# Moving recurrence, layernorm and merge work between engines in a one-core decoder layer

## The chip, the cores and the metric

The kernel runs on one core of one Trainium2 chip. The metric is the device time of one execution in microseconds (us); the profile shows one further execution, taken by the hardware profiler. In profile lines PE is the matmul engine (PEld its weight loads), DVE the vector engine, ACT the activation engine, POOL the GpSimd engine and SP the engine that issues most loads. L158 is line 158 of the kernel before.

## The reference

One layer of a hybrid decoder for 512 prompt tokens and 32 sample tokens (8 sequences of 4), which share all weights. It is computed in float32. The model width is 1024, the hidden width of the MLP 4096.

```python
def _layer(x, states, lp, lb):
    proj = x @ lp["w_in"] + lp["b_in"]          # 15 segments, 51 blocks of 128 columns
    ...
    o, s_gla_new = _gated_linear_scan(q, k, v, g, s_gla)        # 4 heads, dk 48, dv 96
    h_gla = _head_rmsnorm(o, lp["gla_norm_g"]) * jax.nn.silu(gr)
    ...                                                          # mLSTM: 4 heads of 96
    o, s_hg_new = _gated_linear_scan(qh, kh, vh, log_fh, s_hg)  # 4 heads of 64
    h_hg = _head_rmsnorm(o, lp["hg_norm_g"]) * jax.nn.silu(hgt)
    gates = jax.nn.sigmoid(mg)
    merged = (gates[0] * (h_gla @ lp["w_up_gla"]) + gates[1] * (h_ml @ lp["w_up_ml"])
              + gates[2] * (h_hg @ lp["w_up_hg"]))
    x = _layernorm(DN_ALPHA * x + merged @ lp["w_out"], lp["ln1_g"], lp["ln1_b"])
    hid = jnp.square(jax.nn.relu(x @ lp["w_ff_up"]))
    x = _layernorm(DN_ALPHA * x + hid @ lp["w_ff_down"], lp["ln2_g"], lp["ln2_b"])

def _gated_linear_scan(q, k, v, g, s0):          # in chunks, b = cumsum(g)
    rel = exp(where(causal, b[:, :, None] - b[:, None, :], -inf))
    att = sum(q[:, :, None] * k[:, None, :] * rel, axis=-1)
    o = einsum(q * exp(b), s) + einsum(att, v)
    s = exp(b_last) * s + einsum(k * exp(b_last - b), v)
```

## The kernel before, in words

Activations lie with channels on the 128 partitions and the 544 tokens along the free axis, as 8 blocks ("k rows") of 128 channels. Every large product goes through the helper `gemm`. `wload` brings in a weight block of 128 x 1024 as `raw`, ACT copies it to a rounded high part `wh` (L141), and DVE subtracts to get the low part `wl` (L142). For each k row PE then runs three passes (wh with the high activations, wh with the low ones, wl with the high ones), each over two halves of 272 tokens (L158): 48 matmuls for a 1024-deep block. `wh` and `wl` have two buffers each, and so has the PSUM tile `g` of the product. The activations of the layer (`xh`, `xl`), of the MLP's input (`x1h`, `x1l`) and later the last weights (`lh`, `ll`) lie in tiles of `TX` = 546 columns per k row; `x1h` uses the two extra columns for the layernorm's scale and offset.

The program's order is the order of the code, with weight conversion and the emptying of PSUM moved ahead by a priority (`tc.high_priority(OFF)`). It is: the input projections, with the three recurrences run as generators (`together`, `pipe`) whose small matmuls are placed between those of later projections; the three merges, mLSTM first, then GLA, then HGRN2; the output projection with the first layernorm; and twice 16 blocks of the MLP's up product (ff1) followed by its down product (8 output tiles, the last two of which are handled apart at the end, L1066 on).

`gated` is the GLA and HGRN2 recurrence. For each group of tokens, `levels(u)` halves the 128-token chunk again and again: at each level it forms the difference of the cumulative gate `bg` (or `bh`) to the value at the middle of its block, as two subtractions on POOL (L382 for the upper, L384 for the lower half), takes one exponential of the whole tile on ACT (L385), multiplies keys and queries on DVE (L387, L393), lets PE form the scores `lv` (L401) and copies them under a mask into `at` (L405). The diagonal of `at` is written first, from `dps` (PE) over `dsb` (DVE, L364), by one broadcast product on POOL (L367). `sample` brings the states of the eight sample sequences up to date: `spread_v` writes the values eight times under a mask on POOL (L312), POOL scales the state (L503), PE forms `kvs`, DVE adds it (L510).

A `Merge` first runs gate products (`gates`, 48 matmuls each, bias L215, sigmoid in three ACT steps L206 to L208) and then branch products (`products`, 12 matmuls each in the third merge, since HGRN2 has a depth of 256). The product is multiplied by the gate (L868), added to `merged` on POOL (L872), and in the third merge split into `mh` and `ml` for the output projection.

`ln_tile` is called for each of the eight output tiles that a layernorm sums over. It centres on the mean of the first four tiles, before the exact mean and variance are known: tiles 0 to 2 only go into a sum, and at tile 3 PE forms the mean `mu` by a product with `ones5` (1/512), ACT copies it to `cm`, and DVE subtracts it from all four tiles (L972). ACT squares them, POOL adds tile and square to `a1` and `a2` (L978, L979). Later tiles are handled as they come.

Of the kernel before, what the change touches and what calls it, by code (L numbers as in the profile page):

```python
# [42 lines left out]
def build(tc, I, O):  # L43
    nc = tc.nc
    with ExitStack() as ctx:
# [297 lines left out]
        def gated(q, k, b, sc, dv, vtok, sname, nt, gate):  # L343
# [5 lines left out]
            def levels(u):  # L349
# [17 lines left out]
                nc.gpsimd.tensor_tensor(  # L367
                    out=atv, in0=ident[0:R, None, 0:R].to_broadcast([R, 4 * C, R]),
                    in1=dsb[0:R, 0:4 * C, None].to_broadcast([R, 4 * C, R]), op=ALU.mult)

                for li, m in enumerate(LEVELS):
# [10 lines left out]
                    nc.gpsimd.tensor_tensor(out=Ev[:, :, :, m:2 * m], in0=bb[:, :, :, m:2 * m], in1=ref, op=ALU.subtract)  # L382
                    if m > 1:
                        nc.gpsimd.tensor_tensor(out=Ev[:, :, :, 0:m], in0=ref, in1=bb[:, :, :, 0:m], op=ALU.subtract)  # L384
                        nc.scalar.activation(out=E[:, :, 0:L], in_=E[:, :, 0:L], func=AF.Exp, scale=sc)  # L385
                        Kv = K[:, :, 0:L]
                        nc.vector.tensor_tensor(out=blk(Kv)[:, :, :, 0:m], in0=blk(kv)[:, :, :, 0:m], in1=Ev[:, :, :, 0:m], op=ALU.mult)  # L387
                    else:
                        nc.scalar.activation(out=Ev[:, :, :, 1:2], in_=Ev[:, :, :, 1:2], func=AF.Exp, scale=sc)
# [842 lines left out]
```

## Time and profile before

| | us |
|---|---|
| median of 3 runs | 968.91 |
| lowest and highest run | 965.64, 971.26 |
| profiled execution | 968.76 |
| its span (first to last recorded instruction) | 966.9 |
| PE busy | 926.0 (96%) |
| DVE busy | 569.1 (59%) |
| ACT busy | 404.5 (42%) |
| POOL busy | 232.9 (24%) |

The profiled execution's time is the span and 1.9 us around it. The mean granted clock of PE is 0.977 of full speed. PE is busy nearly all the time, so what can be won is the rest: idle stretches of PE, and the time in which its clock is halved behind them. The views used are the page, the groups of instructions by line, the table of stretches (one row per stretch: its start and end, its length, then busy time and count of each engine, the granted clock, the share of the DMA engines and GB/s) and the timeline.

### The profile page before, as it was taken

The page shows a single profiled execution, that of the slowest core. Times are in us where ns is not written, and L with a number is a line of the kernel's source. Part 1 is how long each engine was busy: PE and PEld are TensorE (multiplying, and loading weights), DVE is VectorE, ACT ScalarE, POOL GpSimd, SP SyncE. Part 2 cuts the span into 40 slices and gives each one's busy share as a digit, 9 for nine tenths or more (in the row PEclk, how much of TensorE's full clock was granted, in tenths as well). Part 3 has the DMA queues.
Part 4 walks back from the last instruction along what each step waited for, and adds up shares of the span by engine and source line. Part 5 has one row for each costly group of instructions (what it writes and reads, how often), then busy time and mean ns, then how long its engine had stood idle before and what let it go on. Part 6 is the DMA issues. An engine that isn't in the chain of part 4 may idle for free.

```text
span 966.9 us, 17405 instructions
## 1 busy us (share of the span) xinstructions
PE 926.0 (96%) x7279; PEld 910.7 (94%) x7279; DVE 569.1 (59%) x877; ACT 404.5 (42%) x688; POOL 232.9 (24%) x210
## 2 busy tenths in 40 slices
PE   8999999799999999999989798999999999999795
PEld 7998999799999999999989798999999999999794
DVE  4895467866775676773565855553222455532836
ACT  4386223643555443545523356542111344521414
POOL 0311232643102435120235692000000000001722
PEclk9999999899999999999999899999999999999898
DMA  7321241022132112041144222222222222222202
GB/s 258 118 86 44 84 129 57 16 87 88 60 96 90 49 47 97 25 158 55 33 154 121 79 67 87 88 88 88 87 88 87 88 87 88 88 87 88 85 3 93
DMA packets 37598, 82.73 MB, mean 86 GB/s; under 512 B 12709, under 2 KB 18341, under 8 KB 37521
## 3 DMA queue, kind: packets, MB, share of 16 engines
q1 hardware_dynamic: 25072, 73.28, 23.3%
q10 hardware_dynamic: 12384, 8.33, 3.0%
q8 instruction: 57, 0.93, 0.4%
q14 instruction: 21, 0.16, 0.1%
q0 software_dynamic: 64, 0.02, 0.0%
HBM read 76.51 MB, written 5.09 MB: 84 GB/s over the span
## 4 chain that ended last, share of the span: by engine, by line
PE 86%; DVE 6%; POOL 3%; issue 2%; ACT 1%; DMA 1%; ACTq 0%; DVEq 0%
PE g L158 74%; PE g L83 3%; PE lv L401 2%; POOL merged L1050 2%; POOL merged L1049 1%; DVE wl L142 1%; DVE qe L393 1%; DVE merged L972 1%; PE o L458 1%; DVE x1l L1013 1%; PE oTm L760 1%; PE qkp L673 0%; PE oT L282 0%; DVE ml L180 0%; DMA fw<-in_wfirst 0%
## 5 line engine op out<-in xcount | busy, mean ns | idle before, releaser
L142 DVE TENSOR_TENSOR wl<-raw,wh 128x1024 fp32r<-128x1024 f32 (+2 forms) x139 | 168.4, 1212 | 152.4 <-ACT wh L141 149.6
L141 ACT ACTIVATE wh<-raw 128x1024 fp32r<-128x1024 f32 (+2 forms) x139 | 133.3, 959 | 277.0 <-PE g L158 258.8
L158 PE MATMUL g<-xh,wh 128*128 128x272 f32 x752 | 162.1, 295 | 0.0
L158 PE MATMUL g<-xh,wl 128*128 128x272 f32 x752 | 161.2, 293 | 0.0
L158 PE MATMUL g<-xl,wh 128*128 128x272 f32 x752 | 161.1, 294 | 0.0
L158 PEld LDWEIGHTS g<-xl,wh 128*128 128x128 f32 x752 | 120.8, 191 | 0.9 <-issue 0.5
L158 PEld LDWEIGHTS g<-xh,wh 128*128 128x128 f32 x752 | 121.0, 192 | 0.7 <-issue 0.2
L158 PEld LDWEIGHTS g<-xh,wl 128*128 128x128 f32 x752 | 121.1, 192 | 0.3
L158 PE MATMUL g<-x1h,wh 128*128 128x272 f32 (+1 forms) x512 | 107.1, 290 | 2.9 <-DVE relu L1036 2.9
L158 PE MATMUL g<-x1l,wh 128*128 128x272 f32 (+1 forms) x512 | 106.9, 290 | 0.0
L158 PE MATMUL g<-x1h,wl 128*128 128x272 f32 (+1 forms) x512 | 106.9, 290 | 0.0
L158 PEld LDWEIGHTS g<-x1h,wh 128*128 128x128 f32 x512 | 81.2, 189 | 3.3 <-DVE relu L1036 3.3
L158 PEld LDWEIGHTS g<-x1l,wh 128*128 128x128 f32 x512 | 81.5, 190 | 0.1
L158 PEld LDWEIGHTS g<-x1h,wl 128*128 128x128 f32 x512 | 80.8, 188 | 0.0
L961 POOL TENSOR_TENSOR a<-merged 128x544 f32<-128x544 f32 x2 | 4.8, 2421 | 295.6 <-ACT wh L141 284.3
L158 PE MATMUL g<-hidl,wh 128*128 128x272 f32 x280 | 58.1, 289 | 0.0
L158 PE MATMUL g<-hidh,wh 128*128 128x272 f32 x280 | 57.9, 288 | 0.0
L158 PE MATMUL g<-hidh,wl 128*128 128x272 f32 x280 | 57.8, 288 | 0.0
L1038 ACT ACTIVATE relu<-relu,gw 128x544 f32<-128x544 f32 x32 | 24.0, 750 | 77.2 <-DVE relu L1037 77.2
L872 POOL TENSOR_TENSOR merged<-merged,gb 128x544 f32<-128x544 f32 x16 | 26.8, 1678 | 86.8 <-ACT gb L207 47.8
L215 DVE TENSOR_SCALAR gb<-g,vec 128x544 f32<-128x544 f32 x24 | 18.8, 782 | 45.2 <-PE g L158 45.1
L158 PEld LDWEIGHTS g<-hidl,wh 128*128 128x128 f32 x280 | 44.0, 188 | 0.0
(405 smaller groups left out, 1863.3 us busy)
## 6 DMA issues: line engine op xcount, KB each, us to landing
raw<-in_wff SPq DMA_DIRECT2D x64, 512.0 KB, 3.6
raw<-in_win SPq DMA_DIRECT2D x47, 512.0 KB, 3.2
xr<-in_xT SPq DMA_DIRECT2D x16, 272.0 KB, 3.2
raw<-in_wout SPq DMA_DIRECT2D x8, 512.0 KB, 4.0
out_yT<-merged SPq DMA_DIRECT2D x8, 272.0 KB, 2.4
fw<-in_wfirst ACTq DMA_DIRECT2D x8, 256.0 KB, 5.4
raw<-in_wup_ml SPq DMA_DIRECT2D x8, 192.0 KB, 2.3
raw<-in_wup_gla SPq DMA_DIRECT2D x8, 192.0 KB, 2.4
```

The source lines that it names most:

```text
L83: nc.tensor.matmul(first_ps[i][hf], w[:, i * 128:(i + 1) * 128], a[:, k, hf * HT:(hf + 1) * HT], start=(k == 0 and n == 0), stop=(k == KD ...
L141: nc.scalar.activation(out=h[:, 0:n], in_=raw[:, 0:n], func=AF.Copy)
L142: nc.vector.tensor_tensor(out=l[:, 0:n], in0=raw[:, 0:n], in1=h[:, 0:n].bitcast(F32), op=ALU.subtract)
L158: nc.tensor.matmul(ps[:, hf, 0:w_], w, a(k)[:, hf * HT:hf * HT + w_], start=(k == 0 and s == 0), stop=(k == nk - 1 and s == 2))
L215: nc.vector.tensor_scalar(out, ps, vcol(col), XMIN, ALU.add, ALU.max)
L393: nc.vector.tensor_tensor(out=Q[s, :, p, 0:L // 2].rearrange("p a (n m) -> p a n m", m=m), in0=blk(qv)[s, :, :, m:2 * m], in1=Ev[s, :, :, ...
L401: nc.tensor.matmul(lv[0:R, o:o + 2 * H].rearrange("p (a b) -> p a b", a=2), Kv[:, p, c * R:(c + 1) * R], Q[:, p, :, c * H:(c + 1) * H], st ...
L458: nc.tensor.matmul(o[:, h * dv:(h + 1) * dv], at[:, c * 4 + h, :], vtok[:, cc, h * dv:(h + 1) * dv], start=(h == 0), stop=(cc == 0 and h = ...
L760: nc.tensor.matmul(oT[0:97, h * 32 + 4 * n:h * 32 + 4 * n + 4], Cs[:, n, :], qF[h][:, 4 * n:4 * n + 4], start=False, stop=(h == 3 and n == 7))
L872: eng.tensor_tensor(out=merged[:, m, :], in0=merged[:, m, :], in1=g, op=ALU.add)
L1038: nc.scalar.activation(out=r_, in_=r_, func=AF.Relu, bias=gw[:, 1:2])
L1050: nc.gpsimd.tensor_tensor(out=y, in0=y, in1=rstd, op=ALU.mult)
```

## The change: what it does

1. **Recurrences.** In `levels`, one DVE subtraction over the whole tile takes the place of POOL's two, and the two halves go through two exponentials on ACT, of opposite scale. The diagonal of `at` is written by eight ACT copies (four for the sample tokens), each a 128 x 128 identity scaled by a column of `dsb`. In `sample`, `spread_v` is done by eight ACT copies, and the state is scaled and added to in one DVE instruction per sequence in place of POOL's product and DVE's sum. mLSTM's own calls of `spread_v` stay on POOL.
2. **Layernorms.** They centre on the mean of the first tile alone (`ones7`, 1/128). From tile 0 on every tile is centred when it comes, and the sums `a1`, `a2` are formed on DVE.
3. **Tail.** `ADDP`, `MULP`, `AFFD` are empty: the last additions and products are all on DVE, the last scale and offset all on ACT.
4. **Rows.** `TX` goes from 546 to 548 columns: a k row is 2192 in place of 2184 bytes long.
5. **Third merge.** Gate and branch products alternate, one of each, with one gate ahead, in place of eight gates followed by eight products.

```diff
-TX = T + 2
+TX = T + 4
...
-ADDP, MULP, AFFD = (5, 6, 7), (7,), (2, 5)
+ADDP, MULP, AFFD = (), (), ()
...
-        def spread_v(v, n):
+        def spread_v(v, n, act=False):
             vx = t1.tile([96, 8 * 97], F32R, tag="vx", name="vx", bufs=VXB)
+            if act:
+                for j in range(8):
+                    nc.scalar.activation(out=vx[:, j * n:(j + 1) * n], in_=v.bitcast(F32), func=AF.Copy, scale=bm[0:96, j:j + 1])
+                return vx
...
-                nc.gpsimd.tensor_tensor(
-                    out=atv, in0=ident[0:R, None, 0:R].to_broadcast([R, 4 * C, R]),
-                    in1=dsb[0:R, 0:4 * C, None].to_broadcast([R, 4 * C, R]), op=ALU.mult)
+                for j in range(4 * C):
+                    nc.scalar.activation(out=at[0:R, j, 0:R], in_=ident[0:R, 0:R], func=AF.Copy, scale=dsb[0:R, j:j + 1])
...
-                    nc.gpsimd.tensor_tensor(out=Ev[:, :, :, m:2 * m], in0=bb[:, :, :, m:2 * m], in1=ref, op=ALU.subtract)
                     if m > 1:
-                        nc.gpsimd.tensor_tensor(out=Ev[:, :, :, 0:m], in0=ref, in1=bb[:, :, :, 0:m], op=ALU.subtract)
-                        nc.scalar.activation(out=E[:, :, 0:L], in_=E[:, :, 0:L], func=AF.Exp, scale=sc)
+                        ref2 = bb[:, :, :, m - 1:m].to_broadcast([128, 2, n, 2 * m])
+                        nc.vector.tensor_tensor(out=Ev, in0=bb, in1=ref2, op=ALU.subtract)
+                        nc.scalar.activation(out=Ev[:, :, :, 0:m], in_=Ev[:, :, :, 0:m], func=AF.Exp, scale=-sc)
+                        nc.scalar.activation(out=Ev[:, :, :, m:2 * m], in_=Ev[:, :, :, m:2 * m], func=AF.Exp, scale=sc)
...
+                        nc.vector.tensor_tensor(out=Ev[:, :, :, 1:2], in0=bb[:, :, :, 1:2], in1=ref, op=ALU.subtract)
...
-                    nc.gpsimd.tensor_tensor(
-                        out=Ss[:, :, 0:dv], in0=Ss[:, :, 0:dv],
-                        in1=P[:, p, 0:32].rearrange("p (n m) -> p n m", m=4)[:, :, 3:4].to_broadcast([128, 8, dv]), op=ALU.mult)
...
-                        nc.vector.tensor_tensor(
-                            out=Ss[:, n0:n0 + nb, 0:dv], in0=Ss[:, n0:n0 + nb, 0:dv],
-                            in1=kvs[:, 0:nb * dv].rearrange("p (a b) -> p a b", a=nb), op=ALU.add)
+                        for n in range(n0, n0 + nb):
+                            nc.vector.scalar_tensor_tensor(
+                                Ss[:, n, 0:dv], Ss[:, n, 0:dv], P[:, p, 4 * n + 3:4 * n + 4],
+                                kvs[:, (n - n0) * dv:(n - n0 + 1) * dv], ALU.mult, ALU.add)
...
-        mr_.gates(0, gbp)
-        mr_.gates(4, gb2p)
+        mr_.gates(0, gbp, 1)
         mr_.split()
-        mr_.products(0)
-        mr_.products(4)
-        gb2s.close()
+        for m in range(KD):
+            if m + 1 < KD:
+                mr_.gates(m + 1, gbp, 1)
+            mr_.products(m, 1)
...
-        def ln_tile(x, m, sl, last, after):
+        def ln_tile(x, m, sl, after):
             if m == 0:
-                return
...
+                xr_ = ftile("a1r").bitcast(F32R)
+                nc.scalar.activation(out=xr_[:, sl], in_=x[:, 0, sl], func=AF.Copy)
                 for hf in range(2):
...
+                    nc.tensor.matmul(ps[:, 0:HT], ones7, xr_[:, s], start=True, stop=True)
                     nc.scalar.activation(out=cm[:, s], in_=ps[:, 0:HT], func=AF.Copy)
...
+            nc.vector.tensor_tensor(out=x[:, m, sl], in0=x[:, m, sl], in1=cm[:, sl], op=ALU.subtract)
+            sq = ftile("sq") if m else a2
+            nc.scalar.activation(out=sq[:, sl], in_=x[:, m, sl], func=AF.Square)
+            if after:
+                after(m, sl)
+            if m:
+                nc.vector.tensor_tensor(out=a1[:, sl], in0=x[:, 0, sl] if m == 1 else a1[:, sl], in1=x[:, m, sl], op=ALU.add)
+                nc.vector.tensor_tensor(out=a2[:, sl], in0=a2[:, sl], in1=sq[:, sl], op=ALU.add)
```

The next lists show the order of instructions on one engine, with each row's line, operation, output and inputs, shape and, where it repeats, a count. Rows of the changed kernel carry its own line numbers.

PE before, where GLA's levels for the first 256 tokens begin: `lv` are scores of a level, `oTs` belongs to the sample states, `g` is a projection.

```order
L158 MATMUL g<-xl,wh 128x272 x2
L158 MATMUL g<-xh,wl 128x272
L401 MATMUL lv<-qe_2105,ke_2103 128x128 x4
L489 MATMUL oTs<-at,gvt 96x32 x4
L401 MATMUL lv<-qe_2106,ke_2104 128x128 x4
L498 MATMUL oTs<-qx,Ss 96x2x4 x16
L401 MATMUL lv<-qe_2105,ke_2103 128x128 x4
L158 MATMUL g<-xh,wl 128x272
```

The same place of PE in the changed kernel:

```order
L158 MATMUL g<-xh,wh 128x272
L406 MATMUL lv<-qe_2105,ke_2103 128x128 x4
L158 MATMUL g<-xh,wh 128x272
L158 MATMUL g<-xl,wh 128x272 x2
L158 MATMUL g<-xh,wl 128x272 x2
L158 MATMUL g<-xh,wh 128x272 x2
L158 MATMUL g<-xl,wh 128x272
L494 MATMUL oTs<-at,gvt 96x32 x4
L406 MATMUL lv<-qe_2106,ke_2104 128x128 x4
L503 MATMUL oTs<-qx,Ss 96x2x4 x16
L158 MATMUL g<-xl,wh 128x272
L158 MATMUL g<-xh,wl 128x272 x2
```

Three levels' scores stood behind one another with no projection between them; now projection matmuls stand between them.

DVE before, at tile 3 of the second layernorm: `merged` is the layer's output under way, `a1r` the sum of four tiles that `mu` is formed from, `ll` the last weights.

```order
L1060 TENSOR_TENSOR merged<-merged,g 128x544
L961 TENSOR_TENSOR a1r<-a_5672,merged 128x544
L142 TENSOR_TENSOR wl<-raw,wh 128x1024
L972 TENSOR_TENSOR merged<-merged,cm 128x544 x4
L1075 TENSOR_TENSOR merged<-merged,cm 128x544 x2
L180 TENSOR_TENSOR ll<-raw,lh 128x1024
L142 TENSOR_TENSOR wl<-raw,wh 128x1024
```

DVE in the changed kernel from tile 0 of the second layernorm on:

```order
L1053 TENSOR_TENSOR merged<-merged,g 128x544
L142 TENSOR_TENSOR wl<-raw,wh 128x1024
L965 TENSOR_TENSOR merged<-merged,cm 128x544
L1068 TENSOR_TENSOR merged<-merged,cm 128x544 x2
L142 TENSOR_TENSOR wl<-raw,wh 128x1024
L1053 TENSOR_TENSOR merged<-merged,g 128x544
L965 TENSOR_TENSOR merged<-merged,cm 128x544
L142 TENSOR_TENSOR wl<-raw,wh 128x1024
L971 TENSOR_TENSOR a_5780<-merged 128x544
L972 TENSOR_TENSOR a_5781<-a_5781,sq 128x544
L142 TENSOR_TENSOR wl<-raw,wh 128x1024
```

The block of seven instructions between two weight conversions is gone; at most three now stand there.

DVE in the changed kernel, third merge (before, all L215 with their 1024-wide L142 came first, and then rows such as the last three):

```order
L215 TENSOR_SCALAR gb<-g,vec 128x544
L142 TENSOR_TENSOR wl<-raw,wh 128x1024
L871 TENSOR_TENSOR gb<-g,gb 128x544
L142 TENSOR_TENSOR wl<-raw,wh 128x256
L180 TENSOR_TENSOR ml<-merged,mh 128x544
```

The weight conversion for a gate now falls into the time of a 12-matmul product.

More of the change, by code (lines that the diff above doesn't have):

```diff
@@ L123, in build @@
         nc.gpsimd.memset(epsl, LN_EPS)
-        ones5 = const.tile([128, 128], F32R, name="ones5")
-        nc.gpsimd.memset(ones5.bitcast(F32), 1.0 / 512.0)
+        ones7 = const.tile([128, 128], F32R, name="ones7")
+        nc.gpsimd.memset(ones7.bitcast(F32), 1.0 / 128.0)
         onesn = const.tile([128, 128], F32, name="onesn")
@@ L501, in sample @@
                     yield
-                    vxs = [spread_v(v3[:, (2 * p + e) * dv:(2 * p + e + 1) * dv], dv) for e in range(2)]
-                    nc.gpsimd.tensor_tensor(
-                        out=Ss[:, :, 0:dv], in0=Ss[:, :, 0:dv],
-                        in1=P[:, p, 0:32].rearrange("p (n m) -> p n m", m=4)[:, :, 3:4].to_broadcast([128, 8, dv]), op=ALU.mult)
+                    vxs = [spread_v(v3[:, (2 * p + e) * dv:(2 * p + e + 1) * dv], dv, True) for e in range(2)]
                     for n0 in range(0, 8, nb):
@@ L845, in __init__, with gates @@
                 self.ready = []
-            def gates(self, m0, pl):
-                for m in range(m0, m0 + 4):
+            def gates(self, m0, pl, n=4):
+                for m in range(m0, m0 + n):
                     c = M_G + self.br * KD + m
@@ L861, in split, with products @@
                         split(self.hh[:, k, :], self.hl[:, k, :], self.h[:, k, :])
-            def products(self, m0):
-                for m in range(m0, m0 + 4):
+            def products(self, m0, n=4):
+                for m in range(m0, m0 + n):
                     ps = gemm([(I[self.wup][m], self.nk)], lambda k: self.hh[:, k, :], lambda k: self.hl[:, k, :])
@@ L966, in ln_tile @@
                     s = slice(hf * HT, (hf + 1) * HT)
-                    nc.tensor.matmul(ps[:, 0:HT], ones5, to[:, s], start=True, stop=True)
+                    nc.tensor.matmul(ps[:, 0:HT], ones7, xr_[:, s], start=True, stop=True)
                     nc.scalar.activation(out=cm[:, s], in_=ps[:, 0:HT], func=AF.Copy)
-                nc.gpsimd.memset(a1, 0.0)
-                nc.gpsimd.memset(a2, 0.0)
-            for i in range(0 if m == 3 else m, m + 1):
-                nc.vector.tensor_tensor(out=x[:, i, sl], in0=x[:, i, sl], in1=cm[:, sl], op=ALU.subtract)
-                sq = ftile("sq")
-                nc.scalar.activation(out=sq[:, sl], in_=x[:, i, sl], func=AF.Square)
-                if after:
-                    after(i, sl)
-                eng = nc.vector if last else nc.gpsimd
-                eng.tensor_tensor(out=a1[:, sl], in0=a1[:, sl], in1=x[:, i, sl], op=ALU.add)
-                eng.tensor_tensor(out=a2[:, sl], in0=a2[:, sl], in1=sq[:, sl], op=ALU.add)
+            nc.vector.tensor_tensor(out=x[:, m, sl], in0=x[:, m, sl], in1=cm[:, sl], op=ALU.subtract)
[6 more added lines that the diff above has]
+                nc.vector.tensor_tensor(out=a2[:, sl], in0=a2[:, sl], in1=sq[:, sl], op=ALU.add)
         def ln_sums(hf, stop=True):
@@ L1019, in build @@
             nc.vector.scalar_tensor_tensor(halves(x1[:, m, :]), halves(xr), ALPHA, ps, ALU.mult, ALU.add)
-            ln_tile(x1, m, slice(0, T), m == KD - 1, put_x1)
+            ln_tile(x1, m, slice(0, T), put_x1)
         for hf in range(2):
@@ L1060, in build @@
                     nc.vector.tensor_tensor(out=xm, in0=xm, in1=ps, op=ALU.add)
[L1061 removed]
+                    ln_tile(x1, m, slice(0, T), None)
         lh = bigp.tile([128, KD, TX], F32R, tag="big", name="lh").rearrange("p a b -> p (a b)")
```

8 lines of the change are left out of this document (removed).

## The prediction

> **What bounds the kernel now.** I read the page's totals first, then the table of stretches where PE's busy share drops, then the timeline around each drop.
>
> ```profile
> span 966.9 us, 17405 instructions
> PE 926.0 (96%) x7279; PEld 910.7 (94%) x7279; DVE 569.1 (59%) x877; ACT 404.5 (42%) x688; POOL 232.9 (24%) x210
> PE 86%; DVE 6%; POOL 3%; issue 2%; ACT 1%; DMA 1%; ACTq 0%; DVEq 0%
> ```
>
> PE is the bound. Of the chain that ended last only 14% lies on others, so what any engine can save is PE's idle time and what its clock loses behind that. Stretches (start and end, length, then busy time and count per engine, granted clock):
>
> ```profile
> 170.00:195.00 25.00, 19.66 (x160) 19.02 (x160) 21.94 (x32) 13.83 (x30) 14.65 (x14) 0.80 0.03 9
> 325.00:345.00 20.00, 18.72 (x148) 17.84 (x148) 17.07 (x28) 7.94 (x15) 12.21 (x13) 0.83 0.04 11
> 470.00:500.00 30.00, 24.84 (x177) 23.81 (x177) 22.35 (x29) 12.12 (x23) 12.95 (x9) 0.94 0.33 105
> 530.00:550.00 20.00, 14.72 (x95) 14.31 (x94) 18.08 (x15) 6.48 (x9) 16.06 (x11) 0.83 0.30 93
> 575.00:595.00 20.00, 17.14 (x133) 16.69 (x132) 11.38 (x11) 14.69 (x23) 12.19 (x8) 1.00 0.23 77
> 895.00:920.00 25.00, 19.48 (x134) 19.26 (x133) 22.44 (x16) 9.67 (x14) 18.97 (x11) 0.86 0.27 85
> 430.00:470.00 40.00, 40.00 (x318) 40.00 (x317) 13.11 (x14) 20.51 (x28) 0.00 (x0) 1.00 0.16 54
> 600.00:645.00 45.00, 45.00 (x356) 45.00 (x355) 24.48 (x32) 22.25 (x37) 0.00 (x0) 1.00 0.30 94
> 700.00:745.00 45.00, 45.00 (x361) 45.00 (x360) 12.68 (x12) 8.49 (x8) 0.00 (x0) 1.00 0.27 83
> ```
>
> The last three are undisturbed: 40/318 = 0.126 us per matmul. A stretch of product matmuls alone loses its length less 0.126 x count: the third merge (470 to 500) 7.7 us, the first layernorm (530 to 550) 8.0, the start of ff1 (575 to 595) 3.2, the second layernorm (895 to 920) 8.1. What PE waited for there, in brackets:
>
> ```profile
> 190.52 2.05 PE L401 MATMUL lv<-qe,ke 128*128 128x128 f32 x8 [5.34 <-DVE at L405]
> 336.61 2.07 PE L401 MATMUL lv<-qe,ke 128*128 128x128 f32 x8 [1.28 <-DVE qe L393]
> 491.37 0.52 PE L158 MATMUL g<-mh,wl 128*128 128x272 f32 x2 [2.08 <-DVE wl L142]
> 538.94 0.49 PE L158 MATMUL g<-mh,wh 128*128 128x272 f32 x2 [3.83 <-DVE merged L1019]
> 541.13 0.82 PE L158 MATMUL g<-mh,wl 128*128 128x272 f32 x2 [1.45 <-DVE wl L142]
> 912.99 0.82 PE L158 MATMUL g<-hdh,wl 128*128 128x272 f32 x2 [5.52 <-DVE wl L142]
> ```
>
> The two recurrence stretches mix shapes, so I take gap plus clock. A granted 0.80 over 25 us is 10.0 us at half rate. PE stood for 5.34 of them; the other 4.7 cost half, 2.3; sum 7.7. At 325 to 345 it is 6.8 us at half, 1.28 idle, 2.7 for the rest; sum 4.0. The stretches the change touches hold 7.7 + 4.0 + 7.7 + 8.0 + 8.1 = 35.5 us.
>
> All these waits end on DVE, and in both layernorms DVE was slow while POOL added up tiles (its share of these stretches is in the table above):
>
> ```profile
> 899.82 4.97 DVE L972 TENSOR_TENSOR merged<-merged,cm 128x544 f32<-128x544 f32 x4 [2.42 <-ACT cm L968]
> 904.72 3.68 DVE L1075 TENSOR_TENSOR merged<-merged,cm 128x544 f32<-128x544 f32 x2
> 908.32 2.35 DVE L180 TENSOR_TENSOR ll<-raw,lh 128x1024 fp32r<-128x1024 f32 x1
> 910.59 2.35 DVE L142 TENSOR_TENSOR wl<-raw,wh 128x1024 fp32r<-128x1024 f32 x1
> 914.66 1.21 DVE L142 TENSOR_TENSOR wl<-raw,wh 128x1024 fp32r<-128x1024 f32 x1
> 541.00 0.71 DVE L972 TENSOR_TENSOR merged<-merged,cm 128x544 f32<-128x544 f32 x1
> ```
>
> The same L142 takes 2.35 and 1.21 us, L1075 1.84 each against 0.71 for a like L972. So two things make the layernorm's stall: a block of seven instructions ahead of one `wl`, and POOL's additions beside it.
>
> **Second layernorm (gain 7.6 of 8.1, range 5 to 8.1).** Tile 0's centring no longer waits for tile 3, and no block forms. Each tile of two 1024-deep units is 96 matmuls, 12.1 us, and asks DVE for two `wl` (2.4), the emptying L1060 (0.7 by the like L972) and three subtractions or sums (3 x 0.71): 5.3 us. At tile 0 L1075 comes on top (1.4, without POOL). The new thing at tile 0, the product for `mu`, stands behind the evacuation and an ACT copy; PE has 35 product matmuls (4.4 us) ahead of it, against 0.7 + 0.65 for the two. Lower end 5: another short gap with 3 us of half clock.
>
> **First layernorm (gain 7.5 of 8.0, range 4 to 8).** Tiles are 48 matmuls, 6.03 us. DVE per tile: `wl` 1.21, and L1019, the centring, L1013 and two sums at 0.71 each, by the like shape: 4.8 us, 80% busy, so it keeps up without POOL. The `mu` product has 18 matmuls (2.3 us) of cover.
>
> **Third merge (gain 3 of 7.7, range 0 to 7.7).** Before, eight 12-matmul products of 1.5 us followed one another, each with an L868, a split and a `wl` on DVE; that is gone, since 60 matmuls (7.5 us) now stand for each pair. But a gate's 1024-wide weights can only be converted into the buffer that the gate before it has released, and PE then has just 12 matmuls:
>
> ```profile
> L141 ACT ACTIVATE wh<-raw 128x1024 fp32r<-128x1024 f32 x115 | 121.7, 1058 | 245.4 <-PE g L158 227.3 <-issue 6.4 <-POOL cvo L584 6.3
> L974 ACT ACTIVATE sq<-merged 128x544 f32<-128x544 f32 x14 | 8.9, 649 | 20.0 <-DVE merged L972 18.6 <-POOL a L979 1.3
> ```
>
> [...] PE needs `wl` after 12 + 4 matmuls at 2.1. A stall of 0.55 for each of 6 gates and a like one ahead of the first output block, with 0.4 of aftermath, are 4.3 us, and 7.7 - 4.3 leaves about 3.
>
> **Recurrences (gain 6 of 7.7 and 2 of 4.0; range 0 to 7.7 and -2 to 4).** What POOL did and what takes its place:
>
> ```profile
> L382 POOL TENSOR_TENSOR E<-bg 128x256 f32<-128x256 f32 x14 | 11.1, 798 | 21.9 <-PE oT L282 11.7 <-DVE kw L797 3.4 <-PE dps L361 2.9
> L384 POOL TENSOR_TENSOR E<-bg 128x256 f32<-128x256 f32 x12 | 8.5, 723 | 0.4
> L367 POOL TENSOR_TENSOR at<-ident,dsb 128x1024 f32<-128x1024 f32 x4 | 7.9, 1974 | 9.5 <-DVE dsb L364 9.5
> L416 DVE TENSOR_TENSOR W<-bg 128x512 f32<-128x512 f32 x2 | 1.4, 684 | 0.0
> L389 ACT ACTIVATE E<-E 128x256 f32<-128x256 f32 x4 | 1.7, 428 | 0.0
> L385 ACT ACTIVATE E<-E 128x512 f32<-128x512 f32 x24 | 14.6, 622 | 4.2 <-POOL E L384 4.1
> L699 ACT ACTIVATE D<-dp,cols 128x128 f32<-128x128 f32 x16 | 4.7, 368 | 16.1 <-PE g L158 12.3 <-PE dp L696 3.8
> L474 DVE SCALAR_TENSOR_TENSOR S<-S,P,kvp 64x96 f32<-64x96 f32 x12 | 3.8, 314 | 3.5 <-PE kvp L466 3.2
> ```
>
> Per level 798 + 723 = 1.52 us on POOL and 0.62 on ACT become 0.68 on DVE and 0.86 on ACT: 0.6 us shorter. The diagonal's copies take 8 x 0.294 (16 of L699 in 4.7 us) = 2.35 against 1.97 before. DVE gains 24 x 0.68 + 4 x 0.4 = 18 us of E and, for 32 state updates at about 0.3 against six sums, 6 us; ACT gains 24 x 0.23 + 40 copies for `at` and 64 for `vx` at 0.27 = 34 us. Averaged over the recurrences both have room, and DVE gets back what POOL took from it, as L142 did above. Around 185 us the order now puts 36 projection matmuls instead of 21 between `dps` and the first `lv`, and 8 or 9 behind it, so the chain is covered by 4.5 us and the spacing of levels by 1.1 us. Hence most of the 7.7 goes; at HGRN2, whose gap is small, I take half. Behind it I charge 2 us (0 to 8) for new short waits, where DVE runs up to four E in a row (2.7 us) ahead of a `wl`.
>
> [...]
>
> **Aligned rows (gain 2.5, range 0 to 4.4).** The three undisturbed stretches have 125.8 ns per matmul on `xh` (430 to 470), 126.4 on `x1h` (600 to 645, of which 0.5 are the extra columns) and 124.7 on `hidh` (700 to 745), whose own rows were 2176 bytes, a multiple of 16.
>
> ```profile
> L158 PE MATMUL g<-xh,wh 128*128 128x272 f32 x752 | 162.1, 295 | 0.0
> L158 PE MATMUL g<-x1h,wh 128*128 128x272 f32 (+1 forms) x512 | 107.1, 290 | 2.9 <-DVE relu L1036 2.9
> ```
>
> Excess 1.1 ns on 3 x 752 and 1.2 on 3 x 512 matmuls: 4.4 us if rows of 2184 bytes are the whole cause. Only every second row starts off a multiple of 16, so I take about half. [...]
>
> **ff1 start and tail (0; tail 1 either way).** ff1's stall hangs on POOL's L1049 and L1050, which stay. In the tail
>
> ```profile
> 955.59 4.02 DVE L1099 TENSOR_TENSOR merged<-merged,ne 128x272 f32<-128x272 f32 x5
> 959.53 2.54 DVE L1103 TENSOR_TENSOR merged<-merged,rstd 128x272 f32<-128x272 f32 x7
> 960.00 3.14 ACT L1107 ACTIVATE merged<-merged,vec 128x272 f32<-128x272 f32 x6 [3.31 <-DVE merged L1103]
> ```
>
> five additions beside POOL took 4.02; eight at L1103's 0.36 take 2.9, eight products follow, and eight ACT steps at 0.52 trail them by 4.2 from about 958.9: they end near 963.1, as before.
>
> **Sum.** 7.6 + 7.5 + 3 + 6 + 2 + 2.5 - 2 = 26.6. The profiled execution is 968.76, within 0.2 of the median 968.91, so 968.76 - 26.6 = 942.2, and I say 942.
>
> **Rivals.**
> - *The recurrences keep their stalls.* `at`'s copies queue on ACT behind sigmoids and `wh`, and two more exponentials per level lengthen the chain. For it: the 2.35 against 1.97. Against it: the shorter E and the added cover. Without the 8: 950. Chance 0.2.
> - *The third merge gives everything back.* If each transition stalls 1 us, eight cost 8: gain 0, so 945. Chance 0.1.
> - *All goes.* All 35.5, the rows at their most: 968.8 - 35.5 - 2.5 to 4.4 = about 930. Chance 0.12.
> - *Slower.* DVE becomes the limit of the recurrences: four E and one half E (3.1 us) ahead of an evacuation and `wl`, where only one 18-matmul product (2.3 us) covers them. One such stall costs 1.9 us and up to 2.7 of half clock, 4.6. The other parts bring 20.6, so from the fifth on the kernel loses and from the sixth it ends above 973.6. DVE's 21.94 of 25 us busy in the stretch from 170 speaks for it; that POOL's share leaves that number speaks against. At seven: 980. Chance 0.03.
> - *No effect.* POOL is not what slows DVE, and what moves to DVE takes what the order wins: 966 to 969. The two durations of L142 speak against it. Chance 0.03.
>
> The rest, 0.52, is the forecast. Its own range is 936 to 948; the range that should hold the time goes from all gone with the rows at their most (929) to the first rival with the new waits at their full 8 us (956). A measurement of this kernel tells about 0.5%, 4.8 us, from no change: faster (under 964) 0.94, same 0.03, slower 0.03.
>
> **What would show it.** Right: no gap above 1 us in the two layernorms, granted clock near 1.00 there, L142 and the centring at 1.21 and 0.71 throughout; six short gaps <-DVE wl of about 0.5 us in the third merge; at GLA's start a gap under 1 us; pitch on `xh` near 125. Wrong: gaps released by E subtractions or `at`'s copies in the recurrences, or a granted clock still at 0.8 there, would put the time at 950 or over; a stall of 1 us or more per gate in the merge adds 4; L142 still above 2 us with POOL idle would undo the layernorm steps.

## The result, and the profile after

The changed kernel takes 938.39 us, the median of 4 runs (938.21 to 940.08), against 967.27 for the kernel before in the same series: a ratio of 0.970, 95% interval 0.9664 to 0.9737. It is 28.9 us faster; 942 had been forecast, 26.6 us. A second series gave 936.67, ratio 0.9682 (0.9658 to 0.9707), and is the one that the experiments below stand beside. The profiled execution took 940.08, the highest of the four. In the later series two single executions were far slower (2279.04 us of the kernel before, 1485.51 of the last kernel, at a granted clock of 0.554), and the ratios below leave them out.

The page of the changed kernel (totals, then shares of the chain that ended last):

```profile
span 938.2 us, 17454 instructions
PE 916.5 (98%) x7279; PEld 900.4 (96%) x7279; DVE 556.8 (59%) x959; ACT 437.4 (47%) x824; POOL 101.1 (11%) x92
PE 86%; DVE 5%; POOL 3%; ACT 3%; DMA 1%; issue 1%; POOLq 0%; ACTq 0%; DVEq 0%
```

POOL's work fell by 132 us and ACT's rose by 33. DVE took over whole groups of work, and its busy time still fell by 12: what it no longer loses beside POOL pays for what it took. Its `wl` of 1024 columns went from 1310 to 1270 ns in the mean, the layernorms' centring from 1232 to 723.

The table of stretches of the changed kernel (start and end, length, busy time and count per engine, granted clock): GLA's start, HGRN2's start, a place near 370 that was undisturbed before, the third merge up to the first output block, the first layernorm, the start of ff1, the second layernorm.

```profile
170.00:195.00 25.00, 25.00 (x196) 24.41 (x195) 19.62 (x40) 23.23 (x61) 0.20 (x1) 0.86 0.08 25
325.00:345.00 20.00, 20.00 (x176) 19.21 (x176) 16.77 (x38) 14.30 (x41) 0.00 (x0) 1.00 0.12 32
365.00:375.00 10.00, 8.26 (x71) 7.78 (x70) 7.37 (x14) 5.23 (x13) 4.02 (x3) 1.00 0.29 100
428.00:484.00 56.00, 53.60 (x414) 52.06 (x413) 27.45 (x37) 28.45 (x46) 9.66 (x7) 1.00 0.25 82
485.00:535.00 50.00, 50.00 (x400) 50.00 (x400) 35.62 (x47) 20.63 (x28) 1.71 (x1) 1.00 0.40 125
555.00:575.00 20.00, 16.83 (x132) 16.40 (x131) 12.36 (x12) 12.88 (x21) 14.16 (x8) 1.00 0.25 77
840.00:915.00 75.00, 75.00 (x596) 74.84 (x595) 32.93 (x41) 18.73 (x24) 0.00 (x0) 1.00 0.23 71
```

Both layernorms are now seamless at full clock: 400 matmuls in 50 us and 596 in 75. GLA's start has no idle time left, yet its clock is still 0.86 over 25 us. The start of ff1 is as it was. The gaps that remain in these stretches:

```profile
372.74 0.52 PE L158 MATMUL g<-xh,wl 128*128 128x272 f32 x2 [1.74 <-DVE wl L142]
432.64 0.52 PE L158 MATMUL g<-xh,wl 128*128 128x272 f32 x2 [0.16 <-DVE wl L142]
483.19 0.52 PE L158 MATMUL g<-mh,wl 128*128 128x272 f32 x2 [1.44 <-DVE wl L142]
565.08 0.52 PE L158 MATMUL g<-x1h,wh 128*128 128x272 f32 x2 [1.57 <-DVE relu L1029]
572.99 0.52 PE L158 MATMUL g<-x1h,wh 128*128 128x272 f32 x2 [1.60 <-DVE relu L1029]
```

The first is new. The second is one of six in the third merge, 0.16 each. The third is the step to the first output block, and there a `wl` again stands beside a POOL addition (the timelines of DVE and POOL near it):

```profile
479.80 0.72 DVE L871 TENSOR_TENSOR gb<-g,gb 128x544 f32<-128x544 f32 x1 [0.21 <-PE g L158]
480.69 1.37 POOL L875 TENSOR_TENSOR merged<-merged,gb 128x544 f32<-128x544 f32 x1 [6.11 <-DVE gb L871]
480.76 3.52 DVE L142 TENSOR_TENSOR wl<-raw,wh 128x1024 fp32r<-128x1024 f32 x2 [0.24 <-ACT wh L141]
```

Of the two `wl` in 3.52 us, the first took 2.38, with POOL's addition beside it from 480.69 to 482.06; the second, behind it, took 1.21.

### The profile page after: what moved, and what is told of

It is laid out like the page before. It is cut to its first block, busy times and chain, and to the rows that moved or that the text cites. A ratio compares the mean times of both kernels' runs of the same rounds, so it can differ in the third digit from the quotient of the medians.

```text
span 938.2 us, 17454 instructions
## 1 busy us (share of the span) xinstructions
PE 916.5 (98%) x7279; PEld 900.4 (96%) x7279; DVE 556.8 (59%) x959; ACT 437.4 (47%) x824; POOL 101.1 (11%) x92
## 4 chain that ended last, share of the span: by engine, by line
PE 86%; DVE 5%; POOL 3%; ACT 3%; DMA 1%; issue 1%; POOLq 0%; ACTq 0%; DVEq 0%
PE g L158 73%; PE lv L406 3%; PE g L83 2%; DVE wl L142 2%; POOL merged L1043 1%; ACT wh L141 1%; POOL merged L1042 1%; DMA Cs<-in_mC 1%; PE o L463 1%; POOL cvo L586 1%; PE oTs L503 1%; PE oTm L763 1%; PE qkp L676 0%; DMA fw<-in_wfirst 0%; PE oT L282 0%
## 5 line engine op out<-in xcount | busy, mean ns | idle before, releaser
L142 DVE TENSOR_TENSOR wl<-raw,wh 128x1024 fp32r<-128x1024 f32 (+2 forms) x139 | 158.1, 1138 | 144.0 <-ACT wh L141 142.2
L158 PE MATMUL g<-xh,wh 128*128 128x272 f32 x752 | 159.8, 292 | 0.0
L158 PEld LDWEIGHTS g<-hidh,wl 128*128 128x128 f32 x280 | 43.9, 188 | 0.0
L158 PEld LDWEIGHTS g<-hidh,wh 128*128 128x128 f32 x280 | 43.8, 188 | 0.0
L410 DVE COPY_PREDICATED at<-lmask,lv 128x512 f32<-128x512 int32 (+1 forms) x32 | 26.2, 819 | 22.2 <-PE lv L406 18.2
```

What stands on the lines that cost most here:

```text
L142: nc.vector.tensor_tensor(out=l[:, 0:n], in0=raw[:, 0:n], in1=h[:, 0:n].bitcast(F32), op=ALU.subtract)
L158: nc.tensor.matmul(ps[:, hf, 0:w_], w, a(k)[:, hf * HT:hf * HT + w_], start=(k == 0 and s == 0), stop=(k == nk - 1 and s == 2))
L410: nc.vector.copy_predicated(atv.rearrange("p h (n m) -> p h n m", m=2 * m)[:, :, :, m:2 * m], lmask[0:R, li, 0:H].rearrange("p (n m) -> p ...
```

## The experiments

Differences are to the changed kernel's 936.67 (ratio 0.9682). The runs come from four series, in which the kernel before took 969.10, 967.44, 967.74 and 968.33 us, so a difference of 1 or 2 us can come from the series alone. Two kernels whose intervals overlap are not told apart by their times alone; the traces then say which stretch moved.

| kernel | median us | ratio to before (95%) | difference |
|---|---|---|---|
| changed kernel again | 936.67 | 0.9682 (0.9658 to 0.9707) | 0 |
| rows of 546 columns | 941.04 | 0.9718 (0.9695 to 0.9741) | +4.4 |
| third merge in its old order | 940.66 | 0.9721 (0.9695 to 0.9746) | +4.0 |
| recurrences on POOL | 943.13 | 0.9743 (0.9719 to 0.9768) | +6.5 |
| layernorms as before | 953.39 | 0.9860 (0.9836 to 0.9883) | +16.7 |
| first-tile mean, sums on POOL | 939.95 | 0.9717 (0.9689 to 0.9745) | +3.3 |
| four-tile mean, sums on DVE | 942.38 | 0.9747 (0.9724 to 0.9771) | +5.7 |
| small matmuls spread | 962.71 | 0.9952 (0.9934 to 0.9970) | +26.0 |
| only the subtractions on POOL | 934.62 | 0.9661 (0.9636 to 0.9685) | -2.1 |
| small matmuls in two groups | 936.40 | 0.9678 (0.9651 to 0.9705) | -0.3 |
| own weight tiles, POOL affine | 933.91 | 0.9648 (0.9624 to 0.9673) | -2.8 |
| the two that helped, together | 932.55 | 0.9637 (0.9610 to 0.9665) | -4.1 |

### The changed kernel again

> The changed kernel once more, as the reference for the runs beside it. Expected at its earlier median, 938.4 us, within 1 us; the profiled execution earlier was 940.1.

It came out 1.7 us lower than in the first series; single runs lay between 935.0 and 940.6. The section on the hardware comes back to this spread.

### One part undone at a time

```diff
-TX = T + 4
+TX = T + 2
```

> The changed kernel with rows of 546 columns (2184 bytes) again, all else kept. My theory, from the traces: a matmul on the x tiles whose row starts off a multiple of 16 bytes is slower. The changed kernel's trace has 753 to 755 ns per six matmuls on every row of xh, the one before 765 on every second; over 188 such rows of xh and 128 of x1h that is 11 ns x 316 = 3.5 us, and 0.5 for the rest: slower by about 4 us, 942. The prediction's term was 2.5. Rival: the pitch follows something else (what POOL or the loads do beside it), and the rows are worth nothing: 938 to 939, with all rows alike in the trace.

Measured +4.4, and the rival falls. The same two stretches of both kernels, the changed one first, have 323 against 320 and 320 against 317 matmuls in 40 us:

```profile
25.00:65.00 40.00, 40.00 (x323) 39.96 (x322) 34.60 (x67) 23.27 (x48) 8.66 (x6) 1.00 0.34 110
590.00:630.00 40.00, 40.00 (x320) 40.00 (x319) 22.32 (x28) 19.53 (x34) 0.00 (x0) 1.00 0.29 89
```
```profile
25.00:65.00 40.00, 40.00 (x320) 39.96 (x320) 34.42 (x68) 23.09 (x48) 8.42 (x6) 1.00 0.34 111
590.00:630.00 40.00, 40.00 (x317) 40.00 (x316) 20.55 (x26) 20.92 (x35) 0.00 (x0) 1.00 0.26 82
```

That is 125.0 against 126.2 ns in the second; 1.2 ns over 3792 matmuls are 4.5 us.

```diff
-        mr_.gates(0, gbp, 1)
+        mr_.gates(0, gbp)
+        mr_.gates(4, gb2p)
         mr_.split()
-        for m in range(KD):
-            ...
+        mr_.products(0)
+        mr_.products(4)
```

> The changed kernel with the third merge in its old order (eight gates, then eight products), all else kept. My theory: the old order loses what it lost before, 7.7 us between the last gate and the first output block, against 2.2 in the new order, so slower by 5.5 us: 944. The prediction's term was 3. Rival: part of the old loss came from POOL work and ran into DVE, which is relieved elsewhere, and the short products keep PE fed now: slower by 0 to 2 us.

Measured +4.0, between the two; the spans of the profiled executions differ by 2.5 us only (938.6 against 936.1), so the size is uncertain. The old gaps are back, 0.96, 0.98, 1.03 and 2.09 us, released by `wl` and by L871 as they were before. The stall comes with the order.

```diff
-                        nc.vector.tensor_tensor(out=Ev, in0=bb, in1=ref2, op=ALU.subtract)
-                        ... (two exponentials, eight copies for the diagonal, spread on ACT, eight state updates)
+                    nc.gpsimd.tensor_tensor(out=Ev[:, :, :, m:2 * m], in0=bb[:, :, :, m:2 * m], in1=ref, op=ALU.subtract)
+                        ... (all as in the kernel before)
```

> The changed kernel with the recurrences' work back on POOL (both subtractions, the diagonal, the spread and the state's scaling), all else kept. My theory: both recurrence starts stall again, 14 us lost there before against 5.4 now, but the 1.7 us stall that the changed kernel has near 371 goes: slower by 6 to 8 us, 945. The prediction's terms were 6 + 2 - 2. Rival: the first gap depends on how the order of the projections falls and not on POOL, and the two traces differ by that: slower by less than 3 us or by more than 10.

Measured +6.5. GLA's gap is back to within 0.02 us, as the timeline of PE in this kernel shows, and the gap near 370 is gone:

```profile
191.14 2.04 PE L405 MATMUL lv<-qe,ke 128*128 128x128 f32 x8 [5.36 <-DVE at L409]
```

### Which half of the layernorm's change mattered

> The changed kernel with both layernorms as before (mean of four tiles, catch-up at tile 3, sums on POOL), all else kept. My theory: the two stalls that the trace of before showed come back in full, 8.0 and 8.1 us, so slower than the changed kernel's 936.7 by 15 to 16: 952. Rival: a part of the two stalls was owed to rows or to the state that the recurrences leave, and less than 12 comes back.

Both layernorms as before: +16.7. The gaps of the kernel before stand again, 3.85 and 0.95 in the first, 5.54 in the second. Then each half alone, first the sums on POOL, with the new centring:

```diff
-                nc.vector.tensor_tensor(out=a1[:, sl], ...
-                nc.vector.tensor_tensor(out=a2[:, sl], ...
+                nc.gpsimd.tensor_tensor(out=a1[:, sl], ...
+                nc.gpsimd.tensor_tensor(out=a2[:, sl], ...
```

> The changed kernel, centred on the first tile, but with the sums of both layernorms on POOL again. It parts the two causes that the prediction named, the block at tile 3 and POOL beside DVE. If the block made the stalls: no gap comes back, DVE operations beside POOL take up to twice as long (1.21 to 2.35 for a weight conversion) but DVE has 6.03 us per tile for 3.4 us of work, so at most 1 us slower: 937 to 938. If POOL's company made them: gaps before products in both layernorms, slower by 5 us or more.

No gap came back. Stretches of this kernel, for the first and second layernorm:

```profile
485.00:535.00 50.00, 50.00 (x401) 50.00 (x399) 32.70 (x33) 20.44 (x28) 26.31 (x14) 1.00 0.43 124
840.00:915.00 75.00, 75.00 (x593) 74.68 (x592) 26.43 (x29) 18.49 (x24) 17.78 (x10) 1.00 0.22 71
```

POOL works for 26 of 50 us and PE does not stand. The median is 3.3 us higher, with overlapping intervals, while the profiled span is only 0.8 longer (936.9 against 936.1); whether the sums on POOL cost anything is left open. At the start of ff1 this trace has one gap of 2.15 us in place of two gaps, and the mean granted clock of the execution is 0.989 against 0.991. Then the old centring with the sums on DVE (shown against the layernorms of the kernel before):

```diff
-                eng = nc.vector if m == 3 else nc.gpsimd
+                eng = nc.vector
...
-                eng = nc.vector if last else nc.gpsimd
+                eng = nc.vector
```

> The changed kernel with the four-tile mean and the catch-up at tile 3, but all sums on DVE, none on POOL. If the block makes the stalls: at tile 3 of the first layernorm four tiles of centring, low parts and sums (4 x 2.8 us) stand in DVE's queue, more than a tile's 6.03 us, and at the second 4 x 2.1 us ahead of a weight conversion, so gaps of 2 us and more come back with half clock behind them: slower by 8 to 16, 945 to 953. If POOL's company made them: slower by less than 4.

My expectation for the block fell. At +5.7 the kernel is slower, but not at tile 3: PE has no gap there. DVE's timeline at the second layernorm's tile 3 is the same block as before, with one of the sums in it, at about half the time:

```profile
882.46 2.63 DVE L974 TENSOR_TENSOR merged<-merged,cm 128x544 f32<-128x544 f32 x4 [2.50 <-ACT cm L970]
885.01 1.36 DVE L1077 TENSOR_TENSOR merged<-merged,cm 128x544 f32<-128x544 f32 x2
886.28 0.72 DVE L980 TENSOR_TENSOR a<-a,merged 128x544 f32<-128x544 f32 x1
886.91 1.22 DVE L180 TENSOR_TENSOR ll<-raw,lh 128x1024 fp32r<-128x1024 f32 x1
888.05 1.22 DVE L142 TENSOR_TENSOR wl<-raw,wh 128x1024 fp32r<-128x1024 f32 x1
```

From `cm` to the end of the `wl` it takes 6.8 us (882.46 to 889.27); in the kernel before it took 13.1 (899.82 to 912.94). PE had been fed for 7.7 us behind the arrival of `cm` (899.82 to 907.48). So 6.8 fits and 13.1 does not: the stall needed the block and POOL's company, and either half of the change alone takes it away. What this kernel loses instead is a gap of 2.92 us at the start of ff1, with 3.4 us at half clock behind it (pairs of matmuls start 0.45 us apart from 548.1 to 550.9, where 0.25 is usual); that the late sums of the first layernorm hold up `ne` there is the likely reason, not a tested one:

```profile
546.65 0.53 PE L158 MATMUL g<-x1h,wh 128*128 128x272 f32 x2 [2.92 <-DVE relu L1038]
```

### Which of POOL's works held up the recurrences

```diff
-                        nc.vector.tensor_tensor(out=Ev, in0=bb, in1=ref2, op=ALU.subtract)
-                        ... (two exponentials)
+                    nc.gpsimd.tensor_tensor(out=Ev[:, :, :, m:2 * m], ...
+                        nc.gpsimd.tensor_tensor(out=Ev[:, :, :, 0:m], ...
+                        nc.scalar.activation(out=E[:, :, 0:L], in_=E[:, :, 0:L], func=AF.Exp, scale=sc)
```

> The changed kernel with only the subtractions of the levels back on POOL (two per level, one exponential of the whole tile); the diagonal, the spread and the states stay on ACT and DVE. It asks which of POOL's works made the stall of 5.4 us at GLA's start. If it was POOL's queue (there the diagonal, the spread and the state scaling, 2.2 + 1.9 + 3.3 us, stood among the subtractions): no gap above 1 us near 185, slower than the changed kernel by at most 3 us. If the subtractions themselves on POOL are what is late, or slow DVE beside it: the gap comes back, slower by 5 to 7 us, as with all of it on POOL (943).

With the subtractions on POOL and only the diagonal, the spread and the states off it, no gap above 1 us stands near 185, and the kernel is not slower at all: 934.62. So the subtractions were not the trouble; the other three works were. The expectation would call this POOL's queue, but taking the three off POOL also takes them from DVE's side, and at GLA the trace speaks for the second. What stood on POOL, here with all of it back (the kernel of +6.5), and then with the subtractions only:

```profile
181.04 2.21 POOL L371 TENSOR_TENSOR at<-ident,dsb 128x1024 f32<-128x1024 f32 x1
183.21 1.59 POOL L388 TENSOR_TENSOR E<-bg 128x256 f32<-128x256 f32 x1
184.76 1.95 POOL L316 TENSOR_TENSOR vx<-v,small 96x768 fp32r<-96x768 f32 x1
186.67 3.28 POOL L507 TENSOR_TENSOR Ss<-Ss,P 128x768 f32<-128x768 f32 x2
```
```profile
178.43 2.52 POOL L387 TENSOR_TENSOR E<-bg 128x256 f32<-128x256 f32 x2
185.14 0.67 POOL L385 TENSOR_TENSOR E<-bg 128x256 f32<-128x256 f32 x1
```

In the first, the subtraction that the diagonal delays ends at 184.8 and is next used at 187.91, by the exponential of a later level than the one PE waits for. What PE waits for is a mask copy on DVE (L409), and DVE has no pause there: from 176 to 191 us its instructions follow each other within 0.04 us. They are slow. The DVE instructions of the same work, first with all of it back, then with the subtractions only:

```profile
181.52 2.81 DVE L142 TENSOR_TENSOR wl<-raw,wh 128x1024 fp32r<-128x1024 f32 x1
185.30 1.70 DVE L391 TENSOR_TENSOR ke<-kg,E 128x256 f32<-128x256 f32 x1
187.34 2.90 DVE L397 TENSOR_TENSOR qe<-qg,E 64x256 f32<-64x256 f32 x2
190.27 0.72 DVE L409 COPY_PREDICATED at<-lmask,lv 128x512 f32<-128x512 int32 x1
```
```profile
179.09 1.39 DVE L142 TENSOR_TENSOR wl<-raw,wh 128x1024 fp32r<-128x1024 f32 x1
181.52 0.42 DVE L390 TENSOR_TENSOR ke<-kg,E 128x256 f32<-128x256 f32 x1
181.85 0.85 DVE L396 TENSOR_TENSOR qe<-qg,E 64x256 f32<-64x256 f32 x2
183.94 0.73 DVE L408 COPY_PREDICATED at<-lmask,lv 128x512 f32<-128x512 int32 x1
```

`wl`, `ke` and `qe` take 7.41 us with all of POOL's work beside them and 2.66 with the subtractions only, when POOL is mostly idle (from 180.95 to 184.98). That is 4.75 more, and the gap was 5.36. PE's order differs too, since it is built anew with each edit: with the subtractions only, 12 projection matmuls (1.5 us) follow the 32 small ones. That alone is not the reason, because the mask copy there ends at 184.67, before PE is through with the small matmuls at 184.9. At HGRN2's start POOL's queue does count: with all of it back, the diagonal stands behind four subtractions on POOL, and DVE waits for it:

```profile
333.18 0.73 DVE L409 COPY_PREDICATED at<-lmask,lv 128x512 f32<-128x512 int32 x1 [2.34 <-POOL at L371]
```

Which of the three works weighs most was not tested. The new gap near 370 is absent with the subtractions on POOL. That they are better there is not shown by the times alone (the intervals overlap by half of their width).

### The clock at GLA's start

> The changed kernel with the 32 matmuls of 8 columns (sample states times queries, one burst of 3.6 us at GLA) given a later place, so that they fall in groups of at most ten between projection matmuls; nothing is left out. In the changed kernel the clock is at half from about 188 to 194.5 us although PE is never idle there. If it is this burst that lets the clock fall: the granted clock stays at 1.00 there and the kernel is faster by 2 to 3.5 us, 933 to 935. If the clock falls for another reason (the phase of a clock window after the scores, or idle time that the trace does not show): still half for 6 us somewhere between 180 and 200, and no gain. The matmuls now end later, and if that holds a PSUM buffer too long, a gap before scores appears.

```diff
-                        nc.tensor.matmul(
+                        with tc.high_priority(-2000):
+                            nc.tensor.matmul(
                             ... Ss[:, n, 0:dv], qx[:, p, n], ...
```

The clock is 1.00 from 176 to 238, as the first theory said, and the kernel is 26 us slower: of the burst, at 186 to 189.5 in the changed kernel, 30 matmuls fall between 201.7 and 212.1 and the last two at 239, and the later steps of both recurrences are late with it. Gaps of up to 3.52 us stand between 280 and 303, and others from 415 to 450, released mostly by DVE's work for the recurrences. The edit could not tell what the burst itself costs, so it was made gentler, with the later place for GLA's second state group only (`-(600 * p) if dv == 96 else 0`):

> The changed kernel with GLA's 32 matmuls of 8 columns split in two: the first state group's 16 where they were, the second group's 16 some 80 rows of the order later, with projection matmuls between; HGRN2's unchanged. The earlier split kept the clock at 1.00 but delayed the sample states by 20 us and paid with gaps later. If a burst of 3.6 us lets the clock fall and one of 1.8 us does not: granted clock 1.00 from 180 to 200, and faster by 2 to 3.5 us, 934; the states are late by some 10 us, and if that alone costs gaps further on, slower by up to 10.

The granted clock is 1.00 there again. The gain does not arrive: a gap of 1.50 at 251 takes part of it back, and -0.3 is no difference. But the run with only the subtractions on POOL has the same burst in one piece, and no drop (first the stretch in the changed kernel; then the stretch and the burst in the one with the subtractions on POOL):

```profile
178.00:198.00 20.00, 20.00 (x150) 19.81 (x148) 14.15 (x28) 17.49 (x48) 0.20 (x1) 0.83 0.07 20
```
```profile
178.00:198.00 20.00, 20.00 (x174) 19.84 (x174) 17.46 (x38) 17.44 (x51) 3.78 (x5) 1.00 0.07 20
```
```profile
182.11 2.81 PE L501 MATMUL oTs<-qx,Ss 128*96 128x8 f32 x32
```

So the burst can stand in one piece without a drop. What the traces show of it stands in the last section.

### Towards a better kernel

```diff
-            h = wp.tile([128, 1024], F32R, tag="wh", name="wh")
+            sh, o = ([128, 256], dict(bufs=1)) if nk == 2 else ([128, 1024], dict())
+            h = wp.tile(sh, F32R, tag="wh2" if nk == 2 else "wh", name="wh", **o)
...                                                          # the same for `wl`
-                nc.scalar.activation(out=y, in_=y, func=AF.Identity, scale=vcol(V_L1G + m - 2), bias=vcol(V_L1B + m - 2))
+                nc.gpsimd.tensor_scalar(y, y, vcol(V_L1G + m - 2), vcol(V_L1B + m - 2), ALU.mult, ALU.add)
```

> The changed kernel with two further edits. The third merge's 256-wide branch weights get tiles of their own, so that gate weights alternate between both 1024-wide buffers and can be converted a whole gate ahead: the 0.16 us stalls before each gate and the 1.43 before the output projection should go, 2.5 us. And the scale and offset of the first layernorm's output moves from ACT to POOL, so that ACT's queue no longer waits for POOL at the start of ff1: the gaps of 1.57 and 1.60 should go, 3.2 us. Both: faster by 4 to 5.5 us, 932. Rival for the second: POOL's longer work beside DVE slows DVE's low parts and weights in ff1 so that new gaps take it back, 0 to -3 us.

Measured 2.8 lower, less than expected. The third merge went as expected: the six stalls are gone, and the step to the output block has 0.45 and 0.24 in place of 1.44. At ff1 one of the two gaps stayed:

```profile
557.34 0.52 PE L159 MATMUL g<-x1h,wh 128*128 128x272 f32 x2 [1.59 <-DVE relu L1030]
564.01 0.52 PE L159 MATMUL g<-x1h,wh 128*128 128x272 f32 x2 [0.33 <-DVE relu L1030]
```

The first has another cause than ACT's queue. In the last kernel's timeline of DVE, a `wl` of twice its length stands just ahead of the L1028 that PE waits for, beside POOL's work; that is the rival's mechanism, seen and not tested:

```profile
554.08 2.43 DVE L143 TENSOR_TENSOR wl<-raw,wh 128x1024 fp32r<-128x1024 f32 x1 [2.52 <-ACT wh L142]
556.43 0.77 DVE L1028 SCALAR_TENSOR_TENSOR relu<-ne,gw,g 128x544 f32<-128x544 f32 x1
```

> The changed kernel with what the runs so far found: the levels' subtractions on POOL (as in the run that put only these back, 934.6), own tiles for the third merge's branch weights, and the first layernorm's scale and offset on POOL (together 933.9 in their own run, against 936.7 for the changed kernel beside the first runs). The edits touch different stretches, so the gains should add: 934.6 less 2.5 to 3 us, 931.5 to 932. If less than 1 us is added to the better of the two, they share something, and the trace shows which gap remains.

932.55, ratio 0.9637 (0.9610 to 0.9665), profiled span 929.1. It is the fastest here, 36 us under the kernel before. The gains did not quite add: 2.1 us under the one and 1.4 under the other, and the interval still touches the changed kernel's. The gap near 370 and the six stalls of the merge are gone in its trace.

## Why the prediction was right, and where its terms were not

The four undone parts cost 16.7 + 4.0 + 6.5 + 4.4 = 31.6 us by the medians, and the changed kernel is 32.4 under the 969.1 of its second series: within the scatter of the runs the parts add up, and no large term was overlooked. The 26.6 forecast lies below the 28.9 and 32.4 of the two series, with all four terms on the low side.

- **Layernorms, 7.6 + 7.5 = 15.1.** Measured 16.7. The step was right, its reason included: block and POOL's company were named as two causes, and the runs showed that it took both.
- **Third merge, 3 of 7.7.** Measured 4.0, with overlapping intervals. The 4.3 us that the new order was to lose were met, but by luck: counted the same way, 428 to 484 loses 56 - 414 x 0.125 = 4.25 us. The stall ahead of each gate was put at 0.55, which no run shows, and is 0.16: `wh` and `wl`, 1.06 and 1.21 us, against 2.1 us of matmuls leave 0.17, and the handover adds next to nothing, since `wh` starts at 430.27 and the product behind the gate at 430.32, the buffer of `wh` being free once the passes that use it are through. Against that, the matmuls around such a stall start 0.45 and 0.23 us apart where 0.125 is usual, so each costs 0.43 in all, and the step to the first output block was put at 0.55 and has a gap of 1.44, since its `wl` runs beside POOL (2.38 us against 1.21).
- **Recurrences, 6 + 2 - 2.** Measured 6.5, for reasons that were partly wrong, so the close fit is luck. The 0.6 us that each level was to be shorter is worth nothing here: with the subtractions back on POOL the kernel is as fast. What the change took away was the diagonal, the spread and the state scaling on POOL: at GLA they slowed DVE's operations beside them (7.41 us against 2.66), which the prediction had only as an aside, and at HGRN2 DVE waited for the diagonal, which stood behind the subtractions. GLA's start did not give 6, because 2.3 of its 7.7 was put down to the clock behind the gap, and the clock falls there without a gap: 0.86 over 25 us is 7.0 us at half rate, 3.5 lost, so 4.2 was won. HGRN2 gave all of its 4 in place of 2 in this execution. The charge of 2 for new short waits meets one, 1.74 near 370, though not by a row of E ahead of a `wl`. And a sign of being wrong misled: a clock still at 0.8 was to mean 950 or over, but 178 to 198 has 0.83 in a kernel of 938, as the clock there does not tell of a gap.
- **Diagonal on ACT.** The eight copies were put at 2.35 us, from 16 like instructions (L699) in 4.7, and in this trace eight took 2.45, against 1.97 for POOL's product. At the two starts PE waits for nothing behind these copies. Near 370 they have a part in the gap: ACT waits 2.75 us for `dsb`, DVE then 2.51 us for the copies, and a `wl` further back in DVE's queue starts 1.3 us after its `wh` is done and takes 2.28 beside POOL:

```profile
365.68 2.45 ACT L372 ACTIVATE at<-ident,dsb 128x128 f32<-128x128 f32 x8 [2.75 <-DVE dsb L368]
368.16 0.76 DVE L410 COPY_PREDICATED at<-lmask,lv 128x512 f32<-128x512 int32 x1 [2.51 <-ACT at L372]
370.40 2.28 DVE L142 TENSOR_TENSOR wl<-raw,wh 128x1024 fp32r<-128x1024 f32 x1
```

- **Rows, 2.5 of 4.4.** Measured 4.4. Here the failed step is plain: the excess of 1.1 ns was already a mean over all rows, and halving it because every second row is off counted the same thing twice.
- **ff1 start and tail, 0.** ff1 still has 1.57 and 1.60. The tail went from 11.7 to 11.0 us behind PE's last instruction.

The rivals: the third merge did not give everything back, no engine became the bound, and not all stalls went. The first rival, that the recurrences keep their stalls through ACT's copies, fell: neither start has a gap. Its mechanism has a part in the gap near 370, as the last lines show; how large a part stays open, since with the subtractions on POOL the same copies are there and the gap is not.

## What to carry to other kernels

Where one engine is the bound, price a change stretch by stretch: length less count times the undisturbed pitch. It gave the layernorms within 2 us and showed where nothing was to be had. A stall is a queue against a cover, and what feeds it can be several things at once; undo each alone before saying which it was. An edit that takes work off a queue also takes it away from beside other engines: look at how long the waiting engine's own instructions take before calling it the queue. An average over a group is spread already, so it must not be shared out a second time.
